# The last feature group's down projection by seven block products, with token halves swapped and additions by DMA in place

## The chip, the cores and the metric

The kernel runs on one core of a Trainium2 chip. The metric is the device time in microseconds. Three runs of the kernel before gave 1145.08 to 1145.28, with a median of 1145.26.

The engines are named as in the profile: PE (TensorE) multiplies, PEld is its loading of the stationary operand, DVE is VectorE, ACT is ScalarE, POOL is GpSimd, and SP is SyncE, which only issues DMAs. Each engine takes its instructions in the order in which they were put into its queue.

## The reference, cut to what matters

A trunk of two layers runs over 512 tokens of 1024 features. Each layer normalises x, mixes (layer 0 by a gated short convolution, layer 1 by stick-breaking attention; both also attend to 256 memory tokens), projects the result onto x, and ends with a gated feed-forward block of width 2816. Behind layer 0, x is normalised twice (for the queries of layer 1 and for the shared keys and values); behind layer 1 it is normalised once more and stored.

```python
def swiglu(h, w_gate, w_up, w_down):
    return (jax.nn.silu(h @ w_gate) * (h @ w_up)) @ w_down
...
        x = x + swiglu(rmsnorm(x, ffn_norm[i]), w_gate[i], w_up[i], w_down[i])
...
    return rmsnorm(x, final_norm)
```

All inputs are float32.

## The kernel before, in words

**Three matmuls for one.** Each float32 operand is split in two parts, a high one (a rounding copy on ACT, `hi_of`, L153) and a low one (the rest, a subtraction on DVE, `lo_of`, L156). A product of two operands is then three matmuls: high by high, high by low, low by high (`three`, L345). `split` (L169) does this for weights, in tiles of 128 x 1024 out of a pool of nine buffers; the raw weights come by DMA into a pool of two buffers (`raw_tile`), or into one of two larger ones (`big_tile`). All tiles come from small pools, and a tile's first writer waits until the buffer's last reader is through.

**The feed-forward block** (`ffn`, L797). The 22 feature tiles of 128 are taken as eleven pairs in three groups: pairs 0 to 3, 4 to 7 and 8 to 10 (L40). For each pair, gate and up products are made by feature, with 512 tokens as columns, and `sg` holds silu(gate) x up. At the end of a group, its part of the down projection is added to x (four tiles `xt` of 128 tokens by 1024 features).

**The first two groups** make the down projection by seven block products instead of eight (`seven_products`, L722). The tokens are cut in two halves, the features of a pair in even and odd, and the columns of the weights in two halves. `seven_lhs` (L699) builds the sums and differences of the left operand: e holds A11 and S2, o holds A12 and A22, d holds N1 and S3, n holds N4. On the right, blocks of w_down are summed: T1 and T3 by a plain DMA (`load`, L730, L731) and a second one issued by POOL that accumulates into the same buffer (L733), the others by additions on DVE (`plus`, L753). Each product has two token tiles of 128 rows by 512 columns in PSUM. Some results go to x at once, the others (v, u, w) are kept and added during the next group (`pending`).

**The last group** makes eight block products in the plain way (L834 to L842): for each half of the columns, `by_token` (L396) runs over three pieces of weights and four token tiles, 144 matmuls in all. In the second half the last three pieces are taken tile by tile (`TAIL`), so that a token tile is complete before the next. `residual` (L642) adds the bank to x and takes the squares' sum on ACT; `half` (in layer 1, `gained`, L1011) multiplies the half row by the final gain on DVE; `then` gets the row scale, whose power is taken on POOL (`rstd_of`, L269). In layer 0, `then` is `both_norms` (L862): it scales the row, sets up the transposes for the next projection, and, after tile 1, prepares that projection's weights (`first.prepare`). In layer 1 it is `finish` (L1017): it scales and stores the row.

**What sets the order.** The program is written out by hand, with a small due-time list (`Lanes`, L63) that places the transposes of the norms among matmuls. From it, a scheduler orders each engine's queue when the kernel is built, by the place in the program and by when it reckons operands to be ready. `tc.keep_in_program_order` puts an instruction behind all that was written before it on its engine. `tc.issue_after` puts a block's instructions behind a given one on its engine.

Of the kernel before, what the change touches and what calls it, by code (L numbers as in the profile page):

```python
# [16 lines left out]
P = 128  # L17
# [20 lines left out]
BIG_BUFS = 2  # L38

FF_GROUPS = ((0, 4), (4, 8), (8, 11))  # L40

SEVEN = FF_GROUPS[:2]

TAIL = 3

# [61 lines left out]
def trunk(ctx: ExitStack, tc: tile.TileContext, x, mem, mix_norm, a_in, conv_w, b_in,  # L107
# [36 lines left out]
        lanes.now += P  # L144

    ordered = [True]

    def keep(ins):

        if ordered[0]:  # L150
            tc.keep_in_program_order(ins)
# [2 lines left out]
        keep(nc.scalar.activation(dst, src, AF.Copy))  # L154

    def lo_of(dst, src, hi):  # L156
        keep(nc.vector.tensor_tensor(dst, src, hi.bitcast(F32), ALU.subtract))  # L157


    nw = [0]  # L160
# [535 lines left out]

    def seven_lhs(even, odd, name):  # L699

        h0, h1 = slice(0, 256), slice(256, 512)
        sub = lambda dst, a, b: nc.vector.tensor_tensor(dst, a, b, ALU.subtract)
        diff = t2([P, S], F32, f"ns_{name}")
        n4 = t2([P, 256], F32, f"n4_{name}")
        sub(diff[:, h0], even[:, h1], odd[:, h1])
        sub(diff[:, h1], even[:, h0], even[:, h1])
        sub(even[:, h1], even[:, h0], diff[:, h0])
        sub(n4, odd[:, h0], even[:, h1])
        o, e, d = (split_y(v, f"{name}{n}") for v, n in ((odd, "o"), (even, "e"), (diff, "d")))
        n = slot([P, 2, 256], F32R, f"{name}n")  # L710
        hi_of(n[:, HI, :], n4)
        lo_of(n[:, LO, :], n4, n[:, HI, :])
        home = {"A11": (e, 0), "A12": (o, 0), "A22": (o, 1), "N1": (d, 0), "S3": (d, 1), "S2": (e, 1),
                "N4": (n, 0)}

        def at(operand, hl, t):
            y, hf = home[operand]
            return y[:, hl, hf * 256 + t * P:hf * 256 + (t + 1) * P]

        return at  # L720

    def seven_products(w, g0, lhs, name):  # L722

        n = len(lhs)
        rows4 = w[2 * g0 * P:2 * (g0 + n) * P, :].rearrange("(c two p) n -> p c two n", two=2, p=P)

        def block(i, j):
            return rows4[:, :, i, j * 512:(j + 1) * 512]

        def load(raw, first, second=None):  # L730
            tc.keep_in_program_order(nc.sync.dma_start(raw, block(*first)))  # L731
            if second is not None:
                tc.keep_in_program_order(nc.gpsimd.dma_start(raw, block(*second), accum_op=ALU.add))  # L733
            return raw

        def product(make, operand, raw):
            banks = [make(f"{operand}_{name}{t}") for t in range(2)]
            for c in range(0, n, 2):
                wp = split(raw[:, c:c + 2, :], 2, 512)
                for j in range(2):  # L740
                    for t in range(2):
                        three(banks[t], lambda hl: lhs[c + j](operand, hl, t), lambda hl: wp[hl][:, j, :],
                              c + j == 0, c + j == n - 1)
                        lanes.pump()
            return banks

        def copies(banks):
            held = [t2([P, S], F32, f"v_{name}{t}") for t in range(2)]
# [4 lines left out]
        def plus(dst, raw):  # L753
            for c in range(0, n, 2):
                nc.vector.tensor_tensor(dst[:, c:c + 2, :], dst[:, c:c + 2, :], raw[:, c:c + 2, :], ALU.add)

        def onto(t, hf, v, op=ALU.add):
            part = xt[t][:, hf * 512:(hf + 1) * 512]
            nc.vector.tensor_tensor(part, part, v, op)

        shape = [P, n, 512]
# [3 lines left out]
        v = copies(product(acc, "A11", r1))  # L765
        for t in range(2):
            onto(t, 0, v[t])
        u = copies(product(acc, "N1", r2))
# [28 lines left out]
    def ffn(layer, h, chains, opening, then, half=lambda t, hf: None):  # L797
        ss = sums(f"ssf{layer}")
        pending = []
        for g0, g1 in FF_GROUPS:  # L800
            hid = {}
            seven = (g0, g1) in SEVEN
            for c in range(g0, g1):
                if c == 0:
                    banks = opening.run(h, chains)
                else:
                    gg = cols(w_gate[layer], c * 256)
                    uu = cols(w_up[layer], c * 256)
                for i in range(2):
                    f = 2 * c + i  # L810
                    if c == 0:
                        bg, bu = banks[2 * i:2 * i + 2]
                    else:
                        bg, bu = att(f"g{layer}{f}"), att(f"u{layer}{f}")
# [9 lines left out]
                    if not seven:  # L824
                        hid[f] = split_y(sg, f"hid{layer}{f}")
                    elif i == 0:
                        even = sg
                    else:
                        hid[c] = seven_lhs(even, sg, f"hid{layer}{c}")
            if seven:  # L830
                pending += seven_products(w_down[layer], g0, [hid[c] for c in range(g0, g1)], f"d{layer}{g0}")
                continue
            last = g1 == 11
            for hf in range(2):  # L834
                def done(t, b):
                    residual(t, hf, b, ss if last else None, f"f{layer}{g0}")
                    if last:
                        half(t, hf)
                    if last and hf == 1:
                        then(t, rstd_of(ss[t], f"f{layer}{t}"))  # L840
# [20 lines left out]

    def both_norms(t, r):  # L862
        nq.add(t, xt[t], r)
        if t == 1:
            first.prepare()

    first = Opening(lambda i: acc(f"pb{i}"), lambda: cols(b_in[0], MAIN), lambda: cols(b_in[0], 0))
    ffn(0, h, nh.chains, opening, both_norms)


    key_lo = []
# [1 line left out]
        two = big_tile([P, 2, 2, S], F32R, f"kl{i}")  # L873
        key_lo += [two[:, j] for j in range(2)]
    for kl in key_lo:
        zero_rows(kl)
    qs = [None] * PAIRS
    ks = [None] * PAIRS
    vs = {}
# [129 lines left out]
    xg = {}  # L1009

    def gained(t, hf):  # L1011
        if hf == 0:
# [11 lines left out]
    ffn(1, h, nh.chains, opening, finish, gained)  # L1024


_INS = ["x", "mem", "mix_norm", "a_in", "conv_w", "b_in", "kv_norm", "w_kv_shared", "w_mem_kv",
# [23 lines left out]
```

## Time and profile before

| what | us |
|---|---|
| median of three runs | 1145.26 |
| profiled execution | 1145.12 |
| its span | 1143.4 |
| PE busy | 1130.9 |
| DVE busy | 699.5 |
| ACT busy | 524.1 |
| POOL busy | 76.3 |
| last group's down projection, layer 0, first and last matmul's start | 524.28, 558.46 |
| the same, layer 1 | 1103.80, 1136.21 |

The span runs from the first to the last instruction of the program. All other times are counted from its start. A matmul of 512 columns is shown with 0.39 us, but matmuls overlap; the distance from one start to the next is what a matmul takes of PE. Busy shares are means over the whole span, so a stage is read from a window of its own.

### The profile page before, as it was taken

Reading aid. Unit: us, or ns where it says so; the run is one execution under the profiler, and the core shown is the slowest. Engines: PE = TensorE matmul, PEld = TensorE weight load, DVE = VectorE, ACT = ScalarE, POOL = GpSimd, SP = SyncE. Lnnn points to the kernel's source line nnn. Section 1 sums busy time; section 2 is a strip of 40 time slices with the busy share of each in tenths; the row PEclk is TensorE's granted clock in tenths of the full one; section 3 lists DMA queues with packets and bytes.
Section 4 is the critical chain, followed back from the end, with each engine's and each line's share of the span. In section 5 each row is a group of like instructions: output and inputs, shape, how many; then the busy total and the mean of one; then the engine's idle time right before and its main releaser. Section 6 shows DMA issues by size and latency. Waiting matters only on the chain.

```text
span 1143.4 us, 14862 instructions
## 1 busy us (share of the span) xinstructions
PE 1130.9 (99%) x5844; PEld 963.2 (84%) x5844; DVE 699.5 (61%) x1044; ACT 524.1 (46%) x896; POOL 76.3 (7%) x155
## 2 busy tenths in 40 slices
PE   9999999999999999999999999999999999999997
PEld 9898888988888888888988988788888888888886
DVE  5767453553774468434678799986546844485335
ACT  7555423533432344233666677665434332353223
POOL 1100000000000001000100123321000000000000
PEclk9999999999999999999999999999999999999999
DMA  8332422247332742414222211122274244542311
GB/s 259 111 111 74 144 78 74 74 142 190 111 111 74 219 108 79 141 62 130 75 74 75 74 56 56 38 75 92 74 220 123 66 143 149 109 148 76 126 57 74
DMA packets 97456, 122.10 MB, mean 107 GB/s; under 512 B 2217, under 2 KB 73963, under 8 KB 97387
## 3 DMA queue, kind: packets, MB, share of 16 engines
q1 hardware_dynamic: 93040, 112.73, 30.1%
q0 software_dynamic: 4224, 8.39, 4.3%
q8 instruction: 46, 0.75, 0.3%
q14 instruction: 23, 0.19, 0.1%
q10 hardware_dynamic: 123, 0.03, 0.0%
HBM read 119.05 MB, written 2.10 MB: 106 GB/s over the span
## 4 chain that ended last, share of the span: by engine, by line
PE 92%; issue 3%; DVE 2%; ACT 1%; POOL 1%; DMA 1%; POOLq 0%; ACTq 0%; SPq 0%; DVEq 0%
PE u L136 22%; PE g L136 19%; PE A_d L136 6%; PE d L136 5%; PE o L136 5%; PE N_d L136 4%; PE S_d L136 4%; PE gu L136 4%; PE bg L136 3%; PE v L136 3%; PE k L136 2%; PE pa L136 2%; PE cg L136 2%; PE q L136 1%; PE pb L136 1%
## 5 line engine op out<-in xcount | busy, mean ns | idle before, releaser
L157 DVE TENSOR_TENSOR wl<-raw,wh 128x1024 fp32r<-128x1024 f32 x180 | 220.0, 1222 | 281.3 <-PE u L136 136.5
L154 ACT ACTIVATE wh<-raw 128x1024 fp32r<-128x1024 f32 x180 | 191.0, 1061 | 264.6 <-PE u L136 75.8
L819 ACT ACTIVATE sg<-g 128x512 f32<-128x512 f32 x40 | 23.9, 598 | 105.5 <-PE g L136 105.5
L136 PE MATMUL g<-hffn0h,wh 128*128 128x512 f32 x160 | 62.3, 389 | 0.0
L136 PE MATMUL g<-hffn0l,wh 128*128 128x512 f32 x160 | 62.3, 389 | 0.0
L136 PE MATMUL g<-hffn1h,wh 128*128 128x512 f32 x160 | 62.3, 389 | 0.0
L136 PE MATMUL g<-hffn1l,wh 128*128 128x512 f32 x160 | 62.3, 389 | 0.0
L136 PE MATMUL g<-hffn0h,wl 128*128 128x512 f32 x160 | 62.2, 389 | 0.0
L136 PE MATMUL u<-hffn0h,wh 128*128 128x512 f32 x160 | 62.2, 389 | 0.0
L136 PE MATMUL u<-hffn0l,wh 128*128 128x512 f32 x160 | 62.2, 389 | 0.0
L136 PE MATMUL u<-hffn0h,wl 128*128 128x512 f32 x160 | 62.2, 389 | 0.0
L136 PE MATMUL g<-hffn1h,wl 128*128 128x512 f32 x160 | 62.2, 389 | 0.0
L136 PE MATMUL u<-hffn1h,wh 128*128 128x512 f32 x160 | 62.2, 389 | 0.0
L136 PE MATMUL u<-hffn1l,wh 128*128 128x512 f32 x160 | 62.2, 389 | 0.0
L136 PE MATMUL u<-hffn1h,wl 128*128 128x512 f32 x160 | 62.2, 389 | 0.0
L136 PE MATMUL d<-wh,hid 128*128 128x512 f32 x192 | 59.7, 389 | 0.0
L154 ACT ACTIVATE wh<-b_d 128x1024 fp32r<-128x1024 f32 x32 | 33.7, 1060 | 34.2 <-PE u L136 15.3
L920 DVE TENSOR_TENSOR_SCAN sn<-sn 128x127 f32<-128x127 f32 (+3 forms) x48 | 40.3, 840 | 4.8 <-POOL sn L901 4.4
L136 PEld LDWEIGHTS d<-wh,hid 128*128 128x128 f32 x192 | 36.0, 188 | 7.5
L157 DVE TENSOR_TENSOR wl<-b_d,wh 128x1024 fp32r<-128x1024 f32 x32 | 38.9, 1221 | 4.1 <-PE N_d L136 2.3
L136 PE MATMUL d<-wl,hid 128*128 128x512 f32 x96 | 37.4, 389 | 0.0
L136 PEld LDWEIGHTS u<-hffn0l,wh 128*128 128x128 f32 x160 | 30.0, 188 | 6.3
(777 smaller groups left out, 2937.9 us busy)
## 6 DMA issues: line engine op xcount, KB each, us to landing
raw<-in_w_gate_dram SPq DMA_DIRECT2D x22, 1024.0 KB, 5.3
raw<-in_w_up_dram SPq DMA_DIRECT2D x22, 1024.0 KB, 5.4
raw<-in_w_down_dram SPq DMA_DIRECT2D x12, 1024.0 KB, 6.6
raw<-in_a_in_dram SPq DMA_DIRECT2D x8, 1024.0 KB, 5.5
b_d<-in_w_down_dram SPq DMA_DIRECT2D x8, 1024.0 KB, 7.5
raw<-in_w_o_dram SPq DMA_DIRECT2D x12, 512.0 KB, 3.6
raw<-in_w_kv_shared_dram SPq DMA_DIRECT2D x6, 1024.0 KB, 5.0
raw<-in_w_mem_kv_dram SPq DMA_DIRECT2D x4, 1024.0 KB, 5.2
```

Source lines behind the costliest of these rows:

```text
L136: nc.tensor.matmul(dst, a, b, start=start, stop=stop)
L154: keep(nc.scalar.activation(dst, src, AF.Copy))
L157: keep(nc.vector.tensor_tensor(dst, src, hi.bitcast(F32), ALU.subtract))
L819: nc.scalar.activation(sg, bg, AF.Silu)
L920: nc.vector.tensor_tensor_scan(back, back, back, 1.0, ALU.mult, ALU.bypass)
```

## The change

The last group's down projection is also made by seven block products, in an order of its own (`last_products`). The token halves are swapped for this group: block row 1 is tokens 256 to 511 (x tiles 2 and 3), block row 2 is tokens 0 to 255 (tiles 0 and 1). The order is S2, S3, A11, A22, N1, A12, N4; A22 and N1 complete tiles 0 and 1, A12 and N4 tiles 2 and 3. A22, N1 and N4 are taken tile by tile. All sums of weight blocks are made by accumulating DMAs from POOL: T2 from three blocks, T3 from two; T4 by one more block into T2's buffer, and T1 by a new load and an accumulation in T3's buffer. The results v, w and u go to x in part by accumulating DMAs from SBUF to SBUF (`dma_onto`, 256 KB each), six in all. Some additions are put behind the last low half of the weights of a product (`issue_after`).

Beside this, the preparation of the next projection's weights is called once both tiles 0 and 1 are through, and the memsets of the keys' zero rows are kept behind what was written before them. The first two groups' products move into a class (`Blocks`) with the same instructions.

```diff
-SEVEN = FF_GROUPS[:2]
...
-    def zero_rows(kl):
+    def zero_rows(kl, late=False):
 
         for hh in range(2):
-            nc.gpsimd.memset(kl[HD - hh * HD:P - hh * HD, hh, :].bitcast(F32), 0.0)
+            ins = nc.gpsimd.memset(kl[HD - hh * HD:P - hh * HD, hh, :].bitcast(F32), 0.0)
+            if late:
+                tc.keep_in_program_order(ins)
...
-    def seven_lhs(even, odd, name):
-
-        h0, h1 = slice(0, 256), slice(256, 512)
+    def seven_lhs(even, odd, last, name):
+
+        h0, h1 = (slice(256 * (i ^ last), 256 * (i ^ last) + 256) for i in range(2))
...
+        def more(self, raw, of):
+            tc.keep_in_program_order(nc.gpsimd.dma_start(raw, self.block(*of), accum_op=ALU.add))
...
+        def pieces(self, raw):
+            n = self.n
+            return ((c, split(raw[:, c:min(c + 2, n), :], min(2, n - c), 512)) for c in range(0, n, 2))
+
+        def product(self, make, operand, pieces, by_tile=None):
...
+            if by_tile is not None:
+                pieces = list(pieces)
+                for t in range(2):
+                    banks.append(make(f"{operand}_{self.name}{t}"))
+                    for c, wp in pieces:
+                        piece(c, wp, t)
+                    by_tile(t, banks[t])
+                return
...
+    def dma_onto(t, hf, v):
+        tc.keep_in_program_order(nc.gpsimd.dma_start(x_part(t, hf), v, accum_op=ALU.add))
...
+        r1 = load(big_tile(shape, F32, f"t2_{name}"), (0, 0), (0, 1), (1, 1))
+        r2 = load(big_tile(shape, F32, f"t3_{name}"), (0, 1), (1, 1))
+        r3 = load(raw_tile(shape), (0, 0))
+        r4 = load(raw_tile(shape), (1, 0))
+        v = s.copies(product(acc, "S2", r1), "v")
+        s.more(r1, (1, 0))
+        b3 = product(att, "S3", r2)
+        load(r2, (0, 0), (0, 1))
+        b = product(acc, "A11", r3)
+        r5 = load(raw_tile(shape), (1, 1))
+        w = [t2([P, S], F32, f"w_{name}{t}") for t in range(2)]
+        for t in range(2):
+            nc.vector.tensor_tensor(v[t], v[t], b[t], ALU.subtract)
+            nc.vector.tensor_tensor(w[t], b3[t], v[t], ALU.subtract)
+            dma_onto(t, 0, w[t])
+            dma_onto(2 + t, 1, v[t])
+        for t in range(2):
+            onto(2 + t, 0, b[t])
+        for t in range(2):
+            onto(t, 1, w[t], ALU.subtract)
+
+        def c21(t, b):
+            onto(t, 0, b)
+            squares(t, 0)
+            half(t, 0)
+
+        def c22(t, b):
+            u = t2([P, S], F32, f"u_{name}{t}")
+            with tc.issue_after(before.ins):
+                onto(t, 1, b)
+            squares(t, 1)
+            nc.scalar.activation(u, b, AF.Copy)
+            dma_onto(2 + t, 1, u)
+
+        def c11(t, b):
+            with tc.issue_after(before.ins):
+                onto(2 + t, 0, b)
+            squares(2 + t, 0)
+            half(2 + t, 0)
+
+        def c12(t, b):
+            onto(2 + t, 1, b)
+            squares(2 + t, 1)
+            ended(2 + t)
+
+
+        p4, p1 = list(s.pieces(r1)), list(s.pieces(r2))
+        s.product(att, "A22", p4, c21)
+        p2 = list(s.pieces(r4))
+        before = last_lo[0]
+        s.product(acc, "N1", p1, c22)
+        p3 = list(s.pieces(r5))
+        before = last_lo[0]
+        for t in range(2):
+            ended(t)
+        prepare()
+        for t, b in enumerate(s.product(att, "A12", p2)):
+            c11(t, b)
+        s.product(acc, "N4", p3, c12)
...
-                by_token(w_down[layer], [[2 * c, 2 * c + 1] for c in range(g0, g1)], hf * 512, 512,
-                         ylhs(lambda k: hid[k]), NT, f"d{layer}{g0}{hf}", done, tail=TAIL if last and hf else 1)
+            lhs = [hid[c] for c in range(g0, g1)]
+            if not last:
+                pending += seven_products(w_down[layer], g0, lhs, f"d{layer}{g0}")
+            else:
+                last_products(w_down[layer], g0, lhs, f"d{layer}{g0}", ss, half, then, prepare)
```

## Rows read from the trace of the kernel before

**Rows 1.** The page: busy time of each engine, share of the span, instructions.
```profile
PE 1130.9 (99%) x5844; PEld 963.2 (84%) x5844; DVE 699.5 (61%) x1044; ACT 524.1 (46%) x896; POOL 76.3 (7%) x155
```
**Rows 2.** Busy time by stretch: PE, PEld, DVE, ACT, POOL, clock, DMA share, GB/s.
```profile
524.30:556.90 32.60, 32.60 (x154) 27.24 (x153) 14.98 (x23) 14.00 (x28) 1.66 (x3) 1.00 0.20 65
...
1103.80:1136.40 32.60, 32.60 (x145) 26.84 (x143) 16.58 (x25) 10.03 (x20) 1.66 (x3) 1.00 0.09 33
```
**Rows 3.** Chain of waits, layer 0's last group: start, us, what.
```profile
524.45 28.56 PE d L136 x126
553.01 1.75 PE tr_hmix L143 x16
554.76 4.09 PE d L136 x18
558.85 5.39 PE pb L136 x45
```
**Rows 4.** Layer 1's first matmul and last addition; chain of the tile before.
```profile
1103.80 0.39 PE L136 MATMUL d<-wh,hid 128*128 128x512 f32 x1
...
1136.63 0.69 DVE L645 TENSOR_TENSOR x<-d,x 128x512 f32<-128x512 f32 x1 [1.17 <-PE d L136]
...
1133.34 0.73 ACT junk_f L267 x2
...
1134.39 0.55 POOL rstd_f L273
```
**Rows 5.** Chain of waits, second group's seven products in layer 0.
```profile
420.87 5.46 PE A_d L136 x24
426.34 4.10 PE N_d L136 x18
430.44 2.27 PE S_d L136 x10
...
459.17 2.95 PE g L136 x13
```
**Rows 6.** Timeline of DVE in the same products.
```profile
424.35 0.69 DVE L157 TENSOR_TENSOR hid07e<-sg,hid07e 128x512 fp32r<-128x512 f32 x1
...
437.23 2.36 DVE L157 TENSOR_TENSOR wl<-b_d,wh 128x1024 fp32r<-128x1024 f32 x2
...
455.42 1.89 DVE L759 TENSOR_TENSOR x<-x,v_d 128x512 f32<-128x512 f32 x3
```
**Rows 7.** DMA issues (KB, us to landing); then those of L733 alone (ns to issue).
```profile
raw<-in_b_in_dram SPq DMA_DIRECT2D x4, 1024.0 KB, 5.2
...
raw<-in_w_down_dram SPq DMA_DIRECT2D x4, 512.0 KB, 3.6
out_dram<-out SPq DMA_DIRECT2D x8, 256.0 KB, 2.3
...
L733 POOL DMA_DIRECT2D raw<-in_w_down_dram x4: 1282/1284/1290, 277.6 to 982.2; - x4
...
DMA to landing us min/median/max: 8.4/8.7/9.6
```
**Rows 8.** Timeline of DVE in the first group of layer 0.
```profile
286.05 1.23 DVE L755 TENSOR_TENSOR b_d<-b_d,raw 128x1024 f32<-128x1024 f32 x1 [5.78 <-DMA raw<-in_w_down_dram]
```
**Rows 9.** Timelines of DVE and POOL at the end of layer 0.
```profile
561.63 0.68 DVE L645 TENSOR_TENSOR x<-d,x 128x512 f32<-128x512 f32 x1
...
563.29 1.22 DVE L157 TENSOR_TENSOR wl<-raw,wh 128x1024 fp32r<-128x1024 f32 x1
...
567.21 1.66 DVE L323 SCALAR_TENSOR_TENSOR hmix1l<-tr_hmix,m_cols,hmix1h 128x256 fp32r<-128x256 f32 x4 [0.66 <-ACT hmix1h L321]
...
563.46 1.46 POOL L273 TENSOR_TENSOR rstd_f<-ms_f,minus_half 128x1 f32<-128x1 f32 x1 [8.02 <-DVE ms_f L271]
```
**Rows 10.** Timelines of SP and POOL: the next projection's first load, the memsets.
```profile
530.99 0.37 SPq L181 DMA_DIRECT2D raw<-in_b_in_dram  x1
...
450.21 2.22 POOL L493 MEMSET kl<- 64x512 f32 x4 [8.29 <-DVE wl L157]
```

More of the change, by code (lines that the diff above doesn't have):

```diff
@@ new lines, in at, with __init__, load, block @@
+            c = (h0, h1)[hf].start if y is not n else 0
+            return y[:, hl, c + t * P:c + (t + 1) * P]
+        return at
+    class Blocks:
+        def __init__(self, w, g0, lhs, name):
+            self.lhs, self.name, self.n = lhs, name, len(lhs)
+            self.rows4 = w[2 * g0 * P:2 * (g0 + self.n) * P, :].rearrange("(c two p) n -> p c two n", two=2, p=P)
+            self.shape = [P, self.n, 512]
+        def load(self, raw, first, *more):
+            tc.keep_in_program_order(nc.sync.dma_start(raw, self.block(*first)))
+            for of in more:
+                self.more(raw, of)
+            return raw
+        def more(self, raw, of):
+            tc.keep_in_program_order(nc.gpsimd.dma_start(raw, self.block(*of), accum_op=ALU.add))
+        def block(self, i, j):
+            return self.rows4[:, :, i, j * 512:(j + 1) * 512]
+        def pieces(self, raw):
+            n = self.n
+            return ((c, split(raw[:, c:min(c + 2, n), :], min(2, n - c), 512)) for c in range(0, n, 2))
+        def product(self, make, operand, pieces, by_tile=None):
+            banks = []
+            n = self.n
+            def piece(c, wp, t):
+                for j in range(min(2, n - c)):
+                    three(banks[t], lambda hl: self.lhs[c + j](operand, hl, t), lambda hl: wp[hl][:, j, :],
+                          c + j == 0, c + j == n - 1)
+                    lanes.pump()
+            if by_tile is not None:
[7 more added lines that the diff above has]
+            for t in range(2):
+                banks.append(make(f"{operand}_{self.name}{t}"))
+            for c, wp in pieces:
+                for t in range(2):
+                    piece(c, wp, t)
+            return banks
+        def copies(self, banks, what):
+            held = [t2([P, S], F32, f"{what}_{self.name}{t}") for t in range(2)]
@@ L751, in copies, with plus, x_part, onto @@
             return held
[L753 to L761, printed above, removed]
+    def plus(dst, raw):
+        for c in range(0, dst.shape[1], 2):
+            nc.vector.tensor_tensor(dst[:, c:c + 2, :], dst[:, c:c + 2, :], raw[:, c:c + 2, :], ALU.add)
+    def x_part(t, hf):
+        return xt[t][:, hf * 512:(hf + 1) * 512]
+    def onto(t, hf, v, op=ALU.add):
+        return nc.vector.tensor_tensor(x_part(t, hf), x_part(t, hf), v, op)
+    def dma_onto(t, hf, v):
+        tc.keep_in_program_order(nc.gpsimd.dma_start(x_part(t, hf), v, accum_op=ALU.add))
+    def seven_products(w, g0, lhs, name):
+        s = Blocks(w, g0, lhs, name)
+        load, shape = s.load, s.shape
+        def product(make, operand, raw, by_tile=None):
+            return s.product(make, operand, s.pieces(raw), by_tile)
         r1 = load(big_tile(shape, F32, f"b11_{name}"), (0, 0))
@@ L795, in seven_products, with last_products, product, squares @@
         return left
-    def ffn(layer, h, chains, opening, then, half=lambda t, hf: None):
+    def last_products(w, g0, lhs, name, ss, half, then, prepare):
+        s = Blocks(w, g0, lhs, name)
+        load, shape = s.load, s.shape
+        def product(make, operand, raw, by_tile=None):
+            return s.product(make, operand, s.pieces(raw), by_tile)
+        def squares(t, hf):
+            square_sum(ss[t], xt[t], hf, f"{name}{t}")
+        def ended(t):
+            half(t, 1)
+            then(t, rstd_of(ss[t], f"{name}{t}"))
+        r1 = load(big_tile(shape, F32, f"t2_{name}"), (0, 0), (0, 1), (1, 1))
[16 more added lines that the diff above has]
+            onto(2 + t, 0, b[t])
+        for t in range(2):
+            onto(t, 1, w[t], ALU.subtract)
[26 more added lines that the diff above has]
+        before = last_lo[0]
+        for t in range(2):
+            ended(t)
[3 more added lines that the diff above has]
+        s.product(acc, "N4", p3, c12)
@@ L798, in ffn @@
+    def ffn(layer, h, chains, opening, then, prepare=lambda: None, half=lambda t, hf: None):
         ss = sums(f"ssf{layer}")
@@ L801, in ffn @@
             hid = {}
-            seven = (g0, g1) in SEVEN
+            last = g1 == FF_GROUPS[-1][1]
             for c in range(g0, g1):
@@ L823, in ffn @@
                     del pending[:3]
-                    if not seven:
-                        hid[f] = split_y(sg, f"hid{layer}{f}")
-                    elif i == 0:
+                    if i == 0:
                         even = sg
                     else:
[L829 to L840, printed above, removed]
-                by_token(w_down[layer], [[2 * c, 2 * c + 1] for c in range(g0, g1)], hf * 512, 512,
-                         ylhs(lambda k: hid[k]), NT, f"d{layer}{g0}{hf}", done, tail=TAIL if last and hf else 1)
+                        hid[c] = seven_lhs(even, sg, last, f"hid{layer}{c}")
+            lhs = [hid[c] for c in range(g0, g1)]
[3 more added lines that the diff above has]
+                last_products(w_down[layer], g0, lhs, f"d{layer}{g0}", ss, half, then, prepare)
     def ys(k):
@@ L1011, in gained @@
     def gained(t, hf):
-        if hf == 0:
+        if t not in xg:
             xg[t] = slot([P, D], F32, f"out{t}")
```

37 lines of the change are left out of this document (8 added, 29 removed).

## The prediction, made before the change was run

> **What bounds the kernel now.** The page comes first: TensorE is busy 99% of the span, VectorE 61%, ScalarE 46% [rows 1]. So time is matmuls times their spacing, unless another engine makes TensorE wait. The table by stretches shows the two stages that the change rewrites: TensorE busy 32.60 of 32.60 us in both, clock 1.00, VectorE 15.0 and 16.6 us, ScalarE 14.0 and 10.0 us [rows 2]. The chain of waits runs through them on matmuls alone: 126 in 28.56 us and 18 in 4.09 us, 0.2267 us each, and behind the first stage straight into the next projection [rows 3]. Nothing but TensorE is late there now. Only the end of the second layer is different: the last addition starts at 1136.63, 32.83 us after the stage's first matmul, and the rest of the span, 6.8 us, is that tile's chain [rows 4].
>
> The sum is made against the profiled execution's 1145.12 us (span 1143.4, 1.7 around it); the median of the runs shown is 1145.26.
>
> **What is removed.** A stage has 3 pairs x 2 x 4 token tiles x 2 halves x 3 = 144 matmuls; seven products of 3 pairs x 2 tiles x 3 are 126. 18 x 0.2267 = 4.08 us a layer, 8.16 us in all. Seven products can run without holes: in the second group 168 take 459.17 - 420.87 = 38.30 us against 38.09, because the matmuls of two products are mixed where an operand is late [rows 5]. The new stage begins with S2, whose third pair is due 2.72 us in, while the same operand there was split by 425.04, 4.2 us after u's last matmul; S3's first two pairs can fill this. I charge nothing.
>
> **What is added on VectorE.** Successive 128x512 operations start 0.60 us apart (three in 1.89), 128x1024 splits 1.13 us (two in 2.36) [rows 6]. A product's weights are now 1024 + 512 columns, so 1.73 us of split a product, and 7 x 1.73 = 12.1 us a stage against 6 x 1.22 = 7.3. Call E the end of A11, the third product: 54 x 0.2267 = 12.24 us into the stage. Behind E, VectorE has in order: v and w for two tiles (4 operations), A11 onto x (2), w subtracted (2), splits for N1, then A22's, N1's, A12's and N4's additions with splits for A12 and N4 between.
>
> N1's weights are the first place. T1 is reloaded into the buffer of T3 once S3's second split has read it, 0.65 us into the stage. A plain load of 768 KB lies between 3.6 us (512 KB) and 5.2 (1 MB): 4.3. An accumulating 1 MB took 8.7 in the median [rows 7], 3.5 more than a plain one; 0.9 of that is issue (1.28 for 0.37 [rows 7, 10]) and 2.6 goes with the bytes, so 768 KB is about 7.1. T1 is there 12.1 us in, at E. ScalarE's high half takes 1.06 behind that, and TensorE wants N1's first low half 4.08 + 0.23 = 4.3 behind E. In the program v and w, A11's additions and the subtractions stand ahead of N1's splits: eight operations, to E + 4.8, then 1.13 to E + 5.9, and TensorE has waited 1.6. If the queue has the split first, VectorE idles to E + 1.1, the eight end at 7.1 and the second split, wanted at 4.08 + 1.36 + 0.23 = 5.7, at 7.7: 2.0. If T1 lands 1.3 us earlier the first split runs under A11 and only the second is late: 0.6. Bounds 0.6 and 2.0; I take 1.6, the order of the program.
>
> The in-place additions are the second place. GpSimd issues w0, v0, w1, v1 in this order, 1.28 us each, and A22's additions wait for w0 and w1. No row shows a 256 KB accumulation: a plain one of 256 KB takes 2.3, which is the lower bound, one of 1 MB up to 9.6, the upper [rows 7]. With 0.9 for issue and a quarter of 2.6, I take 3.8. The Trainium skill, in "DMA: Bandwidth & Descriptors", section "Anatomy of one DMA — SWDGE (gpsimd) path", gives about 2.0 us plus the bytes at 436 GB/s: 2.6 us here by that estimate. For 1 MB it gives 4.4 where the trace has 8.4 to 9.6, so an accumulation is not priced by it; with 2.6 the additions would land 1.2 us sooner and rival 3 below would fall away.
>
> With v0 and w0 first, w0 is issued at E + 1.3 and w1 at 3.9; they land at 5.1 and 7.7. VectorE, at N1's second split until E + 6.5, reaches A22's first addition without a wait and the second at 7.1, 0.6 early. Queued behind that one is A12's first split: it ends at 9.4, and TensorE wants it at 8.16 + 1.6 + 0.23 = 10.0. So nothing is lost. In the other order all is 2.3 us later: w1 lands at 10.0, the split behind the second addition ends at 11.7 and TensorE, which wants it at 10.4, waits 1.3. Bounds 0 and 1.3; I take 0. That an order made at build time can take such a transfer as landed too early is seen in the first group: VectorE stood 5.78 us at an addition until it landed, with a split behind it [rows 8].
>
> **Layer 0** then gets 4.08 - 1.6 = 2.5 us, if what follows hides. Before, 16 transposes came 5.8 us ahead of the next projection, and none of its matmuls waited [rows 3]. In the new order tiles 0 and 1 are whole with N1, normalised by about E + 14.5 (addition 0.7, square 0.73, power 0.55 [rows 4], sum, scaling and the steps between), and TensorE has N4 until E + 17.9 and transposes of 1.8 us to cover VectorE's eight low halves (four in 1.66 [rows 9]). Tile 3's addition came 2.8 us after its last matmul before [rows 9], and the first half of the projection, 96 matmuls of 0.12, covered that; it comes no later now. The first b_in load moves from 530.99 [rows 10] to A12's last split, about E + 10.5, lands 5.2 later and is split by E + 18: its cover is N4, and without it some 1 us is lost. The memsets of the keys' zero rows, twice 2.2 us [rows 10], move behind the stage on GpSimd: the query and value projections cover them, and without those they would cost 4.4. The larger loads (11 blocks of 768 KB where two of 1 MB and two of 512 KB stood) meet a DMA share of 0.20 and 0.09 [rows 2]. The first two groups keep their instructions. The extra splits of hidden rows, 1.5 x 0.6 us and four subtractions a pair, lie under 96 gate and up matmuls of 0.2267 us with VectorE at 61%. All of this is charged nothing.
>
> **Layer 1** is bound differently. Besides these operations VectorE multiplies each half row by the gain. Between E and N4's last addition it has 15 additions, 7 gain products (22 x 0.60 = 13.2), six splits (3 x 1.73 = 5.2), three sums (0.6) and two scalings (0.9): 19.9 us, while TensorE is through at E + 17.9. So the last addition starts 12.24 + 19.9 = 32.1 us into the stage against 32.83 [rows 4]: 0.7 gained at most, and each hole in VectorE's queue takes from that. I take 0.5 us of holes: 0.2 us gained. The 6.8 us chain behind it stays.
>
> Sum: 2.5 + 0.2 = 2.7 us, 1145.12 - 2.7 = 1142.4 us. What would be late next is VectorE, not TensorE.
>
> **Rivals.** (1) T1 lands early: N1 waits 0.6 in layer 0, VectorE in layer 1 has no hole, and 0.3 us of scalings slip behind the last addition. 3.5 + 0.7 + 0.3 = 4.5: 1140.6. For it: the group of [rows 5] lost 0.2 us, its accumulated weights were ready. Against it: none of them was reloaded within the stage.
>
> (2) N1's split stands ahead of v and w, and A22's second addition ahead of A12's split. Layer 0: 4.08 - 2.0 - 1.3 = 0.8. Layer 1: VectorE idle 1.1 us behind E and 1.1 (8.9 to 10.0) before the second addition, so 22.1 for 19.9, 34.3 us into the stage: 1.5 lost. In all 0.7 lost: 1145.8. [Rows 8] speak for it, the order of the program against it.
>
> (3) Slower: in that same order the additions in place land late, the place being VectorE in front of A22's second tile. Each further microsecond costs one in each layer. At 6.5 us, near the middle between 3.8 and 9.6, it is 2 x 2.7 = 5.4 more: 1151.2. It makes the kernel slower by over 0.2% from 4.6 us of landing on. For it: 8.7 us at 1 MB. Against: 256 KB is a quarter.
>
> (4) The power on GpSimd lengthens. One took 1.46 us in place of 0.55 while VectorE was in a split [rows 9]; VectorE is now nearly full when the row scales are due. 0.9 in each layer, 1.8 in all: 1144.2. The Trainium skill, "SBUF — State Buffer", section "Who interferes with whom", says that a VectorE instruction with two SBUF inputs holds up a GpSimd one that reads SBUF; the trace agrees with that pair. By it the power at the very end stays short, for by then VectorE has nothing left.
>
> **Chances.** Forecast 0.42, with a range of its own from 1141.0 to 1144.4 (N1's wait 0.6 to 2.0, A12's 0 to 1.3 in layer 0, no hole or 1.1 us in layer 1); rival 1 0.20; rival 2 0.13; rival 3 0.18; rival 4 0.07. A measurement of this kernel tells about 0.2%, 2.3 us, from no change. A little over half of the forecast's chance (0.26) and rival 1 are faster by more: 0.46. The rest of the forecast and rivals 2 and 4 are within it: 0.36. Rival 3: 0.18. The range from 1139.0 to 1147.8 leaves out rival 3 and a little of rival 1, not quite 0.2.
>
> **What would show it.** In the new trace: 126 matmuls where there were 144 in each stage; N1 waiting for a low half of its weights, 16.5 to 18.5 us into the stage, or not; the landing of the 256 KB accumulations; VectorE's wait in front of A22's two additions, and whether A12's split stands between them; VectorE without holes from E to the end in layer 1, and the start of the last addition, 32 us into the stage or earlier. Were the last addition to start at 29 us, VectorE does not bind and the sum for layer 1 is wrong; landings over 4.6 us, or a third late operand, make it wrong on the other side.

## The result, and the profile after

The changed kernel takes 1159.95 us (median; 1157.99 to 1162.99) against 1145.17: a ratio of 1.0132 [1.0109, 1.0154], slower, and far outside the predicted range. Its profiled execution is the slowest of its runs, 1162.99 us; against the 1145.12 of before it lost 17.9 us. Three readings of the two traces place them. The stage in layer 0 begins 0.6 us later (524.87 for 524.28). From there to the first q matmul of the next projection it takes 68.9 us where it took 59.2: 9.7 lost. In layer 1, from the stage's first matmul to the end of the span, 47.2 where it took 39.6: 7.6 lost. As the 36 matmuls that went are worth 2 x 4.08, something took 13.8 and 11.7 us.

The page says that TensorE is no longer the only thing that is late: busy 98%, on fewer matmuls than in [rows 1], and VectorE with 33 us more.

```profile
PE 1132.8 (98%) x5808; PEld 959.4 (83%) x5808; DVE 732.7 (63%) x1112; ACT 540.7 (47%) x932; POOL 101.3 (9%) x177
```

The table by stretch, columns as in [rows 2], shows where: TensorE is busy 6.20 of 10.70 us while N1 runs, and the granted clock, 1.00 there before, is under 1 in each of the later stretches shown. The last three rows are narrow stretches at or near the lower level (1.2 of 2.4 GHz), each behind one of TensorE's waits.

```profile
524.90:541.50 16.60, 16.60 (x73) 13.15 (x71) 8.37 (x14) 7.44 (x12) 1.26 (x1) 1.00 0.58 143
541.50:552.20 10.70, 6.20 (x20) 4.42 (x19) 8.17 (x13) 2.83 (x6) 3.57 (x4) 0.86 0.58 98
564.40:593.80 29.40, 26.53 (x210) 26.32 (x209) 22.77 (x44) 21.51 (x45) 6.70 (x10) 0.94 0.34 110
...
1131.00:1151.80 20.80, 15.74 (x54) 11.66 (x54) 17.65 (x29) 9.20 (x20) 6.42 (x8) 0.84 0.49 91
...
549.60:552.20 2.60, 2.60 (x8) 2.00 (x6) 0.88 (x2) 0.84 (x4) 0.00 (x0) 0.50 0.99 172
569.20:573.20 4.00, 3.99 (x21) 3.99 (x21) 3.51 (x8) 4.00 (x11) 2.10 (x3) 0.57 0.01 5
1138.30:1143.00 4.70, 4.70 (x13) 3.62 (x11) 2.39 (x5) 2.13 (x6) 0.00 (x0) 0.50 0.76 129
```

The chain of waits through layer 0's stage held matmuls alone [rows 3]. Now it leaves TensorE as the stage begins and comes back 44 us later. Each line is start, duration, what: T1's plain load, its accumulation, ScalarE's high half, VectorE's low half, v and w, an in-place addition, A12's split, and at last the load of b_in.

```profile
525.63 4.55 DMA t_d<-in_w_down_dram
530.22 0.50 issue
530.72 9.58 DMA t_d<-in_w_down_dram
540.40 1.07 ACT wh L153
541.49 1.23 DVE wl L156
542.72 1.19 DVE v_d L870 x2
...
545.97 5.26 DMA x<-w_d
...
551.93 0.52 DVE wl L156
...
559.08 8.64 DMA raw<-in_b_in_dram
...
569.21 8.22 PE pb L134 x54
```

VectorE's timeline shows what was queued behind the late operand: it stands 7.38 us in front of N1's first split, then does v, w and x, and only then the second split, which N1 needs 1.36 us after the first. A12's split stands behind an addition that waits 2.31 us for w1.

```profile
541.49 1.23 DVE L156 TENSOR_TENSOR wl<-t_d,wh 128x1024 fp32r<-128x1024 f32 x1 [7.38 <-ACT wh L153]
542.64 1.28 DVE L870 TENSOR_TENSOR v_d<-v_d,A_d 128x512 f32<-128x512 f32 x2
...
546.22 1.28 DVE L792 TENSOR_TENSOR x<-x,w_d 128x512 f32<-128x512 f32 x2
547.43 0.68 DVE L156 TENSOR_TENSOR wl<-t_d,wh 128x512 fp32r<-128x512 f32 x1
548.33 0.69 DVE L792 TENSOR_TENSOR x<-x,A_d 128x512 f32<-128x512 f32 x1 [0.22 <-DMA x<-w_d]
551.32 0.69 DVE L792 TENSOR_TENSOR x<-x,A_d 128x512 f32<-128x512 f32 x1 [2.31 <-DMA x<-w_d]
551.93 1.22 DVE L156 TENSOR_TENSOR wl<-raw,wh 128x1024 fp32r<-128x1024 f32 x1
```

Behind the stage it is ScalarE: a split of b_in waits for its load, and the transposed rows that the projection needs are queued behind it.

```profile
567.74 1.06 ACT L153 ACTIVATE wh<-raw 128x1024 fp32r<-128x1024 f32 x1 [3.60 <-DMA raw<-in_b_in_dram]
568.70 0.82 ACT L321 ACTIVATE hmix1h<-tr_hmix,m_cols 128x256 fp32r<-128x256 f32 x2
```

TensorE's rows give the waits themselves, two in N1 and one in the projection. From the start of one matmul to the next, less the 0.23 us that a matmul takes, N1's are 1.0 and 3.9 us; the profile's own figures are smaller because it shows a matmul longer than that.

```profile
541.54 0.47 PE L134 MATMUL N_d<-wh,hid08d 128*128 128x512 f32 x1
542.77 0.50 PE L134 MATMUL N_d<-wl,hid08d 128*128 128x512 f32 x1 [0.77 <-DVE wl L156]
...
544.04 0.39 PE L134 MATMUL N_d<-wh,hid010d 128*128 128x512 f32 x1
548.16 0.50 PE L134 MATMUL N_d<-wl,hid010d 128*128 128x512 f32 x1 [3.74 <-DVE wl L156]
...
569.21 0.50 PE L134 MATMUL pb<-hmix1h,wh 128*128 128x256 f32 x2 [2.87 <-ACT hmix1h L321]
```

Layer 0's 13.8 us are then: N1's two waits 1.0 + 3.9 = 4.9; 2.60 us at half clock 1.3; A12 0.9, and behind it 0.8 until the rows to be transposed are there; the projection's wait 2.9 and its matmuls at 0.57 of the clock 4.0 x 0.43 = 1.7; 1.3 is spread. This is the longest of the four runs; which of these losses the one at 1157.99 had less of, no trace shows. Layer 1's last addition answers to [rows 4]; it starts 1154.07 - 1114.09 = 40.0 us into the stage in place of 32.8.

```profile
1131.05 1.23 DVE L156 TENSOR_TENSOR wl<-t_d,wh 128x1024 fp32r<-128x1024 f32 x1 [7.70 <-ACT wh L153]
...
1140.87 0.69 DVE L792 TENSOR_TENSOR x<-x,A_d 128x512 f32<-128x512 f32 x1 [2.31 <-DMA x<-w_d]
...
1154.07 0.68 DVE L792 TENSOR_TENSOR x<-x,N_d 128x512 f32<-128x512 f32 x1
```

### The profile page after: what moved, and what is told of

It is laid out like the page before. It is cut to its first block, busy times and chain, and to the rows that moved or that the text cites. A ratio compares the mean times of both kernels' runs of the same rounds, so it can differ in the third digit from the quotient of the medians.

```text
span 1161.3 us, 14987 instructions
## 1 busy us (share of the span) xinstructions
PE 1132.8 (98%) x5808; PEld 959.4 (83%) x5808; DVE 732.7 (63%) x1112; ACT 540.7 (47%) x932; POOL 101.3 (9%) x177
## 4 chain that ended last, share of the span: by engine, by line
PE 85%; issue 4%; DMA 4%; DVE 3%; POOL 2%; ACT 1%; POOLq 0%; ACTq 0%; DVEq 0%
PE u L134 22%; PE g L134 19%; PE A_d L134 6%; PE o L134 5%; PE N_d L134 4%; PE S_d L134 4%; PE gu L134 4%; PE bg L134 3%; PE v L134 3%; DMA t_d<-in_w_down_dram 2%; PE pa L134 2%; PE pb L134 2%; PE q L134 2%; PE cg L134 2%; PE k L134 2%
## 5 line engine op out<-in xcount | busy, mean ns | idle before, releaser
L156 DVE TENSOR_TENSOR wl<-raw,wh 128x1024 fp32r<-128x1024 f32 (+1 forms) x180 | 216.4, 1203 | 249.5 <-PE u L134 118.5
L153 ACT ACTIVATE wh<-raw 128x1024 fp32r<-128x1024 f32 (+1 forms) x180 | 187.9, 1045 | 237.6 <-PE u L134 79.7
L743 POOL DMA_DIRECT2D t_d<-in_w_down_dram x14 | 18.1, 1363 | 580.7 <-DMA t_d<-in_w_down_dram 316.8
L156 DVE TENSOR_TENSOR wl<-t_d,wh 128x1024 fp32r<-128x1024 f32 (+1 forms) x24 | 25.1, 1045 | 48.7 <-PE u L134 22.3
L153 ACT ACTIVATE wh<-t_d 128x1024 fp32r<-128x1024 f32 (+1 forms) x24 | 21.7, 914 | 53.1 <-DMA t_d<-in_w_down_dram 24.0
```

The costliest lines, as they stand in the source:

```text
L156: last_lo[0] = nc.vector.tensor_tensor(dst, src, hi.bitcast(F32), ALU.subtract)
L743: tc.keep_in_program_order(nc.gpsimd.dma_start(raw, self.block(*of), accum_op=ALU.add))
```

## The experiments

A is the time from layer 0's first matmul of the stage to q's first, B that from layer 1's to the end of the span; last is the start of the last addition and V the end of VectorE's last operation, both in us into B. All four are from the profiled execution, us. That execution is not always near the median: 3.0 us above it for the changed kernel, 1.1 below for e12.

```
run             median us   ratio to before [95%]      A      B     last   V
before          1145.2      -                          59.2   39.6  32.8   35.7
changed         1159.95     1.0132 [1.0109, 1.0154]    68.9   47.2  40.0   43.5
e1_order        1148.54     1.0029 [1.0018, 1.0039]    59.5   41.2  34.0   37.5
e2_early        1148.76     1.0028 [1.0016, 1.0039]    60.0   42.0  34.3   37.8
e3_dve_adds     1160.53     1.0132 [1.0116, 1.0147]    64.7   47.8  40.7   44.2
e4_layer1       1153.61     1.0073 [1.0058, 1.0088]    59.2   47.5  40.3   43.8
e5_r5_late      1158.37     1.0114 [1.0098, 1.0129]    65.5   46.0  38.4   41.8
e6_early_a12    1147.41     1.0016 [1.0007, 1.0025]    61.8   39.6  31.9   35.4
e7_order_a12    1145.61     1.0003 [0.9994, 1.0012]    58.4   40.1  32.4   35.9
e8_early_dve_w  1144.67     0.9994 [0.9985, 1.0003]    57.6   39.9  32.8   36.3
e9_both         1144.62     0.9994 [0.9985, 1.0002]    57.9   39.9  32.8   36.2
e10_pool_gain   1147.39     1.0018 [1.0009, 1.0027]    57.6   42.7  34.5   38.8
e11_no_dma_adds 1148.06     1.0023 [1.0014, 1.0031]    58.9   42.4  35.3   38.8
e12_w_dma       1146.4      1.0005 [0.9996, 1.0014]    58.8   39.7  30.8   35.7
e13_no_gain     1144.81     0.9995 [0.9986, 1.0004]    58.8   38.4  31.2   34.6
e14_w_dve       1146.0      1.0005 [0.9996, 1.0014]    59.9   39.5  30.7   35.5
e15_tail        1144.36     0.9994 [0.9985, 1.0003]    57.7   39.5  29.3   35.8
```

**The order of VectorE's queue, or the landing.** Four kernels take the suspects one at a time. The first moves N1's splits only:

```diff
-            onto(t, 1, w[t], ALU.subtract)
+            sub = onto(t, 1, w[t], ALU.subtract)
...
+        with tc.issue_after(sub.ins):
+            p1 = list(s.pieces(r2))
```

> Edit: the low halves of N1's weights stand behind the eight operations on v, w and x in VectorE's queue; loads and accumulating DMAs as they are. Theory (T1's accumulation lands 3 us after A11's end, and everything queued behind N1's first split waits with it): VectorE does the eight operations while T1 is on its way, the first low half is there about 18.2 us into the stage, N1 loses about 1.6 us in place of 6.5 and 7.4: 10 to 12 us less than the changed kernel, 1148 to 1150 us. Rival A (the in-place additions by DMA are what costs): N1's wait only moves, A12's grows, 1156 to 1160 us. Rival B (VectorE has too much work, whatever the order): 1158 to 1160 us.

Measured 1148.54. T1 still lands 9.69 and 9.73 us after its issue, yet 11.4 of the 14.8 us are back. The timeline of VectorE shows the eight operations done while T1 is on its way, and no wait in front of the split:

```profile
536.94 0.69 DVE L870 TENSOR_TENSOR v_d<-v_d,A_d 128x512 f32<-128x512 f32 x1 [2.87 <-PE A_d L134]
...
540.53 1.28 DVE L792 TENSOR_TENSOR x<-x,w_d 128x512 f32<-128x512 f32 x2
541.74 1.82 DVE L156 TENSOR_TENSOR wl<-t_d,wh 128x1024 fp32r<-128x1024 f32 x2
543.47 0.68 DVE L792 TENSOR_TENSOR x<-x,A_d 128x512 f32<-128x512 f32 x1
545.63 0.69 DVE L792 TENSOR_TENSOR x<-x,A_d 128x512 f32<-128x512 f32 x1 [1.48 <-DMA x<-w_d]
```

The second leaves the order and takes the late landing away; T1 and A12's block change places:

```diff
-        r4 = load(raw_tile(shape), (1, 0))
+        r4 = load(raw_tile(shape), (0, 0), (0, 1))
...
-        load(r2, (0, 0), (0, 1))
+        load(r2, (1, 0))
...
```

> Edit: T1 is built ahead of the stage, in a staging buffer, and A12's plain block is what is reloaded into T3's buffer; VectorE's order as it is, N1's splits ahead of v and w. Theory: no landing is late for N1, its 6.5 and 7.4 us go, what stays is A12 (1 to 1.7 us a layer) and the projection behind layer 0 (4.6 us): 1145 to 1149 us. Rival A (in-place additions): 1155 to 1160 us. Rival B (VectorE's work): layer 1's last addition still starts 40 us into its stage, 1157 us or more.

Measured 1148.76: N1 has no wait, A12 has 1.9 and 2.8 us. Either cure alone is worth the same 11 us: it needs a late operand and work queued behind it. The third takes the accumulations in place away instead (`dma_onto` calls `onto`):

> Edit: the six in-place additions of a stage are VectorE instructions in the same places instead of accumulating DMAs (3.6 us more VectorE work a stage); T1 is reloaded as in the changed kernel. Theory: N1's wait stays and its second split, with four more operations ahead of it, comes 2.4 us later; A22's second addition no longer waits 2.3 us: 1158 to 1164 us. Rival A (the in-place additions by DMA are what costs): N1 loses under 2 us, 1147 to 1150 us. Rival B (VectorE's work): 1166 us or more, 3.6 us a layer on top.

Measured 1160.53; TensorE's waits for N1's weights, by the profile's figures for both layers, are 10.6 us in the trace, 9.0 in the changed kernel. So the additions in place are not what costs most. A is 4.2 us shorter all the same: the b_in loads take 5.1 to 5.4 us there. The fourth keeps the old last group in layer 0.

> Edit: block products for the last feature group in the second layer only; the first layer's last group goes token by token as before the change. If the losses of the two layers are separate: the second layer's loss alone, 7.6 us over the kernel before, 1152 to 1154 us. If the second layer's loss hangs on what the first one leaves behind (the clock, queues, the loads of the projection between them): 1146 to 1150 us.

Measured 1153.61, 8.3 over before: the two layers lose separately. A is that of before, and B is 0.3 us from the changed kernel's.

**Why T1 took 9.6 to 9.9 us.** N4's block waits for a one-column memset behind N1's split:

```diff
-        r5 = load(raw_tile(shape), (1, 1))
+        r5 = raw_tile(shape)
...
+        with tc.issue_after(last_lo[0].ins):
+            tc.keep_in_program_order(nc.vector.memset(r5[:, 0, 0:1], 0.0))
+        load(r5, (1, 1))
...
```

> Edit: the changed kernel, but the plain 768 KB load of N4's block, which it issues 0.9 us behind T1's accumulation, starts only behind N1's second split (a one-column VectorE memset of that buffer holds it back). Theory C (T1's accumulation took 9.6 to 9.9 us instead of the predicted 7.1 because that load runs beside it; alone such an accumulation took 7.2 to 7.5): T1 lands after 7.2 to 7.6 us, N1 is 2.2 us earlier in each layer, 1154 to 1157 us. Rival (an accumulation on the way to a waiting consumer just takes 9.7): landing 9.5 us or more, 1159 to 1162 us.

The landing is as theory C said, 7.31 us (the row is of the chain of waits) and 7.45 in layer 1:

```profile
531.03 7.31 DMA t_d<-in_w_down_dram
538.44 1.07 ACT wh L153
```

The time, 1158.37, missed 1154 to 1157. N1 is 2.2 and 4.4 us shorter, but what it gave in layer 1 went to the next late operand: A12 takes 10.05 us there in place of 5.14, 3.0 of it a wait for its split behind A22's second addition, and the granted clock is 0.66 in it.

**What e2 still loses.** Both splits of A12 go ahead of A22's second addition:

```diff
+            if t == 1:
+                p2.extend(s.pieces(r2))
+                with tc.issue_after(last_lo[0].ins):
+                    onto(t, 0, b)
...
```

> Edit: T1 built ahead of the stage as in the run before with that edit, and A12's two splits moved ahead of A22's second addition in VectorE's queue. Theory (what that run, 1148.8 us, still loses is A12's 2.8 us wait, which comes from its splits standing behind an addition that waits 2.3 us for w1's accumulation, and the clock behind it): no wait of TensorE over 0.5 us in either stage, VectorE's 2.3 us hole filled, last addition of layer 1 about 31 to 32.5 us into its stage: 1141.5 to 1144.5 us, faster than the kernel before. Rival B (VectorE's work binds): layer 0 gains 3 us, layer 1 nothing: 1145 to 1147 us.

Measured 1147.41, a miss. No product waits for weights in either stage, but a cost of layer 0 that I had not seen apart stands out: two b_in loads land 9.64 and 7.89 us after issue, with accumulations in place in flight beside them, and ScalarE waits for the second with the transposed rows behind it, as in the changed kernel. The eleven runs of e6 lie between 1144.53 and 1149.37, and the profiled one took 1148.09, so this cost need not be in every run.

```profile
560.06 1.06 ACT L153 ACTIVATE wh<-raw 128x1024 fp32r<-128x1024 f32 x1 [2.80 <-DMA raw<-in_b_in_dram]
561.02 1.19 ACT L321 ACTIVATE hmix1h<-tr_hmix,m_cols 128x256 fp32r<-128x256 f32 x3
```

The same order on top of e1's, T1 still late:

> Edit: T1 late as in the changed kernel, with both orders mended: N1's splits behind the eight operations, A12's splits ahead of A22's second addition. Theory (a late landing costs little once nothing is queued behind it): N1 still loses 1.1 us, A12 nothing; 1144 to 1146.5 us. If the landing itself costs, whatever the order: 1147 us or more.

Measured 1145.61, as expected: with nothing queued behind it, a 9.9 us landing costs N1 1 us. In e8, w0 and w1 are added by VectorE (`onto(t, 0, w[t])` for `dma_onto`); e9 joins this to e6's order.

> Edit: T1 built ahead of the stage, and w added to the left half rows by VectorE (two more 0.6 us operations a stage) instead of by accumulating DMAs; A12's splits stay behind A22's second addition. Theory (the in-place addition costs by its landing, 5.3 us from issue, not by work): the 2.3 us hole turns into 1.2 us of work, A12's first low half is 1 us earlier than with the hole; 1144 to 1147 us. If VectorE's work binds, layer 1 gains under 0.5 us over 1148.8: 1147 to 1149 us.

> Edit: T1 built ahead of the stage, w added to x by VectorE, and A12's splits ahead of A22's second addition: nothing that TensorE waits for stands behind an accumulation. Theory (layer 1 is bound by VectorE's work between A11 and the last addition, layer 0 by TensorE): layer 0 gains 0.4 us over the run with w by VectorE alone (A12's wait), layer 1 nothing although TensorE's 1.3 us wait there goes: 1143.5 to 1145 us. Rival (TensorE's waits bind both): 1142 to 1143 us.

Measured 1144.67 and 1144.62, both as expected, though layer 0 is not 0.4 us shorter in e9 than in e8. It gains 1.3 to 1.6 us over before, layer 1 nothing, though e9 has no wait of TensorE over 0.2 us there. With all six additions on VectorE:

> Edit: T1 built ahead of the stage, A12's splits ahead of A22's second addition, and none of the six in-place additions of a stage by DMA: VectorE does all of them (3.6 us more a stage than by DMA). Theory (an accumulating DMA in place saves VectorE 0.6 us and costs by its landing and by slowing loads beside it): the loads for the projection behind layer 0 take 5.1 to 5.5 us in place of 7.9 to 9.6, TensorE waits about 1 us for N1's second split, and layer 1's last addition is 2.4 us later than with w alone by VectorE: 1145.5 to 1148 us. If contention of the transfers is the larger cost: 1144 us or less.

Measured 1148.06, 0.06 over the range: the loads behind layer 0 take 5.1 to 5.5 us, and VectorE's work costs more than that gives. The loads' median in the two traces, e6 and then e11 (KB each, us to landing):

```profile
raw<-in_b_in_dram SPq DMA_DIRECT2D x4, 1024.0 KB, 7.2
```

```profile
raw<-in_b_in_dram SPq DMA_DIRECT2D x4, 1024.0 KB, 5.3
```

So no load is late in e11, which has no accumulations there. But an accumulation beside a load is not enough to make it late. In the changed kernel and in e1, u's two accumulations are issued 3.1 and 1.5 us ahead of the second b_in load, and it takes 8.6 us in the one and 5.5 in the other (5.6 in e7). What decides between them is not shown. The second load in the changed kernel, then in e1:

```profile
raw<-in_b_in_dram SPq DMA_DIRECT2D x1, 1024.0 KB, 8.6
```

```profile
raw<-in_b_in_dram SPq DMA_DIRECT2D x1, 1024.0 KB, 5.5
```

**What binds layer 1.** GpSimd multiplies the gain for tiles 0 and 1 (`eng = nc.gpsimd if t < 2 else nc.vector`):

> Edit: as the run before it in this set, and the final norm's gain is multiplied onto tiles 0 and 1 by GpSimd in layer 1 (four of VectorE's eight 128x512 gain products, 2.4 us). Theory (VectorE's work binds the end of layer 1): the last addition starts about 2 us sooner, 31 us into the stage instead of 33, 1.5 to 2.2 us less than that run: 1141.5 to 1143 us. Rival (the chain at the end binds, or GpSimd holds VectorE up): within 0.5 us of that run, or slower.

Measured 1147.39, slower. A gain product takes GpSimd 1.89 us, the row scales' powers are queued behind four of them, VectorE's scaling waits for those, and N4's second split is queued behind the scaling; TensorE waits 3.6 us. It is the changed kernel's fault once more, so it tells nothing of the binding.

```profile
1131.58 1.03 DVE L1135 TENSOR_SCALAR out<-out,rstd_d 128x512 f32<-128x512 f32 x2 [3.59 <-POOL rstd_d L273]
1132.53 0.69 DVE L156 TENSOR_TENSOR wl<-raw,wh 128x512 fp32r<-128x512 f32 x1
```

Three kernels put N4's splits ahead of the row scales (`with tc.issue_after(before.ins): ended(t)`). e12 and e14 leave GpSimd two gain products and scale tiles 0 and 1 on ScalarE; e13 leaves out the four gain products.

> Edit: T1 built ahead of the stage, A12's splits ahead of A22's second addition, w by VectorE in layer 0 and by accumulating DMA in layer 1; in layer 1 GpSimd multiplies the gain onto the left halves of tiles 0 and 1 only, ScalarE scales these two tiles whole, and N4's splits stand ahead of their row scales. VectorE has 17.8 us of work between A11 and the last addition by the prediction's rows. Theory (layer 1 is bound by VectorE's work, and the run with four gain products on GpSimd lost by N4's split queued behind a row scale, not by the binding): last addition 30 to 31 us into the stage, no wait of TensorE over 0.5 us, 1141.5 to 1143.5 us, faster than the kernel before. Rival (GpSimd's gain products, 1.89 us each in that run, hold up VectorE or u's accumulations): 1144.5 us or more.

> Edit: as the first run of this set, but w by VectorE in layer 1 too (1.2 us more work, no accumulation that A22's additions wait for). Theory (VectorE's work binds, landings hidden behind A12's splits cost nothing): 0.5 to 1.2 us more than that run, 1142.3 to 1144.5 us. If landings still cost: less than that run.

> Edit: the run with w by VectorE and both orders mended (1144.6 us), with the gain products of tiles 0 and 1 left out of layer 1 altogether (four of eight, 2.4 us of VectorE's work; their rows come out without the final norm's gain), and N4's splits ahead of their row scales. Theory (VectorE's work binds layer 1): 1.8 to 2.4 us less, 1142.2 to 1142.8 us. Rival (the chain behind the last addition or TensorE binds): 1144 to 1145 us.

Measured 1146.4, 1146.0 and 1144.81 (one run of e12, at 6430 us, is left out): three misses in the time, with e12 and e13 in the ranges of their rivals; e14 is 0.4 us under e12, less than either's runs scatter. Last additions at 30.7 to 31.2 us are within 0.8 us of the count of VectorE's work ahead of them (30.0, 31.2 and 30.9). But e12 and e14 lost that again, their four scalings on ScalarE standing ahead of the last squares; in e13, B fell by 1.5 us and A rose by 0.9, since layer 0's row scales too now stood behind N4's splits (with them in their old place, e15 has A at 57.7). The last run keeps layer 0's order, puts layer 1's additions first and the final norm behind them:

```diff
+            with tc.issue_after(tail[0].ins):
+                for t in (1, 0):
+                    half(2 + t, 0)
+                    ended(2 + t)
+                then(1, r[1])
```

> Edit: T1 built ahead of the stage; A12's splits ahead of A22's second addition; w by VectorE in layer 0, by accumulating DMA in layer 1; layer 0's row scales where the run with both orders mended has them. In layer 1 the last additions come first in VectorE's queue and the final norm behind them: tiles 0 and 1 get row scale and gain in one VectorE operation each half (no separate gain and no ScalarE scaling), tiles 2 and 3 their gains behind the last addition, tile 3 ahead of tile 2. Theory (layer 1 is bound by what stands in VectorE's queue ahead of the last addition): that addition starts 29.5 to 31 us into the stage in place of 32.8, the end comes 1 to 2.5 us sooner than with both orders mended alone (1144.6 us): 1141.5 to 1143.5 us, faster than the kernel before. Rival (all of VectorE's work, wherever it stands, binds the end): the last addition comes sooner but the end doesn't, 1144 us or more.

Measured 1144.36, and the rival holds: the last addition is 3.5 us earlier than before the change, and the end is not, because VectorE's remaining work only moved behind it, with 0.9 us of waits for two row scales' powers among it. VectorE's rows in that stage, which starts at 1103.15:

```profile
1132.48 0.68 DVE L792 TENSOR_TENSOR x<-x,N_d 128x512 f32<-128x512 f32 x1
...
1138.23 0.75 DVE L1156 SCALAR_TENSOR_TENSOR out<-x,rstd_d,g_final 128x512 f32<-128x512 f32 x1
```

V, VectorE's end, is 35.8 us here, 36.2 in e9, 35.7 before the change, and under 35 in e13 alone, which leaves work out; the span ends 3.6 to 4.2 us behind it in every run. No version beats the kernel before by more than its interval; the best three are 0.06% under it.

## Why the prediction was wrong

**The step that failed** is N1's wait, "Bounds 0.6 and 2.0; I take 1.6, the order of the program". In layer 0 it was 4.9 us, and 6.6 with the clock (7.4 in layer 1). Two terms made it. The landing: 7.1 us is right for that transfer alone (7.31 and 7.45 in e5), but I had not looked at what SP issues beside it; with N4's 768 KB load in flight it took 9.58 and 9.89. T1 was there 3.2 us behind E (540.30 - 537.11), not at E. The order: the queue had the first split ahead of v and w. I priced that at 2.0, but with T1 at E. With E + 3.2, the first low half is done at E + 5.6 and the second split, behind eight operations, at E + 11.0, where TensorE wanted it at 5.7: 5.3 late, against which TensorE was itself 0.3 behind. Each term alone costs little (e7, and e2 for the other side); I had bounded them one by one, and the price is in their product.

**In-place additions.** 3.8 us was taken; w0 to v1 landed after 3.42, 4.31, 5.26 and 6.01, as their issues overlap, 0.91 to 1.88 us each. VectorE's order was the one of rivals 2 and 3, and the mechanism is rival 3's, at 5.3 us rather than 6.5, with A12 losing 0.9 and 1.1 us. It was the smaller part: e3, without them, is no faster. Rival 3's 1151.2 is 8.8 us short too, mostly since N1 loses 2.0 in it.

**Charged at nothing.** "lands 5.2 later" was 8.64 us for the second b_in load, with u's accumulations in flight, and "without it some 1 us is lost" was 2.9 of wait and 1.7 of clock. Why this load was late stays open (e1 and e7 have it at 5.5 and 5.6). That a transfer beside another costs could be read before the change: there a 1 MB load of w_down took 5.0 us alone and 6.4 to 7.2 beside an accumulation. One of each:

```profile
raw<-in_w_down_dram SPq DMA_DIRECT2D x1, 1024.0 KB, 5.0
```

```profile
raw<-in_w_down_dram SPq DMA_DIRECT2D x1, 1024.0 KB, 6.4
```

TensorE's clock was no term of the sum at all: behind three waits of 2.9 to 3.9 us, what came next ran at about half, 1.2 GHz of 2.4, for 2.6, 4.0 and 4.7 us; 1.3 + 1.7 + 2.4 = 5.4 us over both layers. The 0.6 us ahead of the stage, charged at nothing too ("The first two groups keep their instructions"), comes in two steps of 0.3 us, one in each of these groups' seven products; the gate and up products with the hidden rows' extra splits lose nothing. e4, which has none of these splits in layer 0, shows the same two steps. What makes them was not tested.

**What held.** 126 matmuls a stage. That layer 1 is bound by VectorE: without holes the last addition was to start at 32.1 us; e6, with the same work, has 31.9, e9, with 1.2 us more, 32.8, and in e13, with 2.4 us less than e9, B is 1.5 shorter. In the changed kernel the holes behind E are 4.7 + 0.2 + 2.3 us and 0.5 for a row scale's power, 7.7 in place of 0.5, and 32.1 + 7.7 = 39.8 against the 40.0 measured. So layer 1's gain is nothing, as 0.2 said, and B's 7.6 us are VectorE's holes. Layer 0's 2.5 us would have been 1.3 to 1.6 in good order (e8, e9). The change, mended, is worth 0.7 to 0.9 us (e8, e9, e15), and each interval reaches past no change.

## What to carry to other kernels

Bound a late operand together with its place in the consumer's queue: one landing 3 us late became 4.9 us of wait in each layer, 6.6 and 7.4 with the clock, because eight other operations stood between the two halves of a split. Where the order is made at build time, price the order that hurts with the landing that hurts, and look for every transfer that is issued beside the one that is due. An engine that is one wait away from binding, as VectorE in layer 1, takes the whole gain of the engine that you relieve.

## What the runs showed of the hardware

- A plain 1 MB load of b_in takes 5.1 to 5.5 us where the stage has no accumulations (e3, e11), and 5.0 to 9.6 where accumulations of 256 KB are in flight beside or just ahead of it (5.5 and 5.6 in e1 and e7, 8.6 in the changed kernel, 7.9 and 9.6 in e6). An accumulation of 768 KB from HBM takes 7.3 to 7.5 us alone, in some runs 8.4 to 8.5 at one place in layer 1 (changed kernel, e1), and 9.6 to 9.9 with a plain load of 768 KB issued 0.9 us later. With another accumulation 0.8 us ahead of it, it takes 10.4 to 10.8 (e2, e6, e9), and 14.8 with a plain load beside both (changed kernel).
- Accumulating DMAs that GpSimd issues 0.5 to 0.6 us apart take 0.91, 1.19, 1.53 and 1.88 us to issue (changed kernel).
- GpSimd multiplies 128x512 f32 by 128x512 in 1.29 to 2.20 us (e12), and two splits of VectorE's beside it took 2.92 in place of 1.82; in e10 the same two took 1.82 beside it, and the next split 1.79 in place of 1.22. The Trainium skill, "SBUF — State Buffer", section "Who interferes with whom", says that this pair of operand kinds contends; e12's trace agrees, and shows that VectorE can pay too; that it does not each time is e10's.
- The granted clock was 1.00 through a 2.8 us wait of TensorE in N1 (e5, 1128.0 to 1135.1) and fell to about half behind a 2.9 us one in the projection (changed kernel) and a 3.0 us one in A12 (e5); which of such waits it falls behind, no run here shows.
